# Half a head's scores inside the next half's query projection, and a new order of the routing's work on VectorE, in a product-key expert layer

## The chip, the cores and the metric

One Trainium2 chip, one core. The metric is the device time of one execution in microseconds (us). The kernel before takes 1438.37 us (median of three runs, 1434.36 to 1438.52).

## What is computed

One block for 512 tokens of width 1024, in float32: `h = x + W_out [gated MLP group ; chunked attention group](RMSNorm(x))`, then `out = h + PEER(RMSNorm(h))`. PEER is a layer of 16384 experts, of which each token uses 8 x 16. The routing is what the change touches:

```python
q = (xb @ w_query).reshape(PEER_TOKEN_BLOCK, PEER_HEADS, 2, PEER_HALF)
sc = jnp.einsum('thpd,hpkd->thpk', q, sub_keys).astype(jnp.float32)
s_top, i_top = lax.top_k(sc, PEER_TOPK)
cand = s_top[:, :, 0, :, None] + s_top[:, :, 1, None, :]
cand_idx = i_top[:, :, 0, :, None] * PEER_NKEYS + i_top[:, :, 1, None, :]
...
best, pos = lax.top_k(cand, PEER_TOPK)
eidx = jnp.take_along_axis(cand_idx, pos, axis=-1)
g = jax.nn.softmax(best, axis=-1)
...
return jnp.einsum('thk,thkd->td', (g * h.astype(jnp.float32)).astype(xb.dtype), vv)
```

There are 8 heads; a head has two halves, each with 128 sub-keys of length 128. For each token and half the 16 best sub-keys are taken, the 50 pairs that can be among the best 16 sums are formed, and the best 16 of these give the experts' numbers and the gates.

## The kernel before

**The whole.** Three of the four tiles of 128 tokens (384 tokens) go densely through all experts: TensorE multiplies every expert row, and a gating stage between the two products writes each token's gates at its experts. One tile, and 64 tokens of the last dense tile in the first product, fetch their experts' rows by indirect DMA instead. A float32 product is three products of split parts ("high" and "low"): `mm3`. Each weight block arrives as `raw` (512 KB, queue SP), ScalarE writes its high part `hi` (L151), and GpSimd or VectorE the low part `lo` (L152). There are 3 raw, 5 hi and 5 lo buffers, handed on in order, so a load and its splits can be at most a few blocks ahead of TensorE.

**Stages.** In the profile the routing runs from about 224 to 442 us, the gating stage to about 606, and the last stage, with the second expert product, to the end.

**The routing, loop over h = 0 to 8 (L863 and after).** `candidates(h)` (L803) projects the head's two halves, 24 products of 512 columns each (tile `pa` from `xbh`, `xbl`), and copies each half to SBUF on ScalarE (`qt`, L820). Then come the first of the head's fill tiles and the scores of both halves, 8 products of 128 columns on TensorE (L828), which ScalarE copies to `scr` (L831). A fill tile is 24 products of 320 columns for the first expert product (`pu`, `first_products`, L716 for its activation `act`, L713); the table FILL says how many a head gets, and they give TensorE something to do beside the choice. VectorE takes the top 16 of each half (`top16`, L729 to L733: three tiles of tokens, five instructions each).

One loop turn later follows head h - 1: `pairs` (L744) copies the first half's values and positions and adds the pairs (`cand`, L764); for all heads but the last two of these turns, ScalarE does the copies (L750, L756, L757). `choose` (L769) spreads the candidates' numbers into `tree` (L771, on ScalarE; on VectorE for the last two heads), takes the top 16 of the candidates, makes six bit masks of the positions (L778, one instruction for each bit) and picks with `COPY_PREDICATED` by each bit (L788), down to `eidx` (L790).

**Row products.** From h = 2 on, the chosen indices of head h - 2 go to GpSimd (`eui`, L665, L666), which issues indirect DMAs of expert rows, six at a time into six buffers `rowe` (L650). In the next turn VectorE multiplies each with the token row `xbu` (L659, 128 x 1024, with the sum to `du`). A buffer is free for the next gather when its product is done.

**The end of the routing.** Turn h = 8 has no projection but a "bridge" of 8 fill tiles. Then one further tile is multiplied and the digits of the chosen numbers, `ii` (L843 to L850, from the last `eidx`), are transposed on TensorE (L918), with which the gating stage begins: VectorE makes one-hots (`hb`, `lb` L929, `am` L948), GpSimd their products (`bm`, L940).

**What sets the order.** Outside of the gating stage a scheduler places the instructions of each engine in its queue, by the order in which the code names them and by their dependences; `issue_after` and `queued_behind` hold instructions behind a given one. The queues run in order: an instruction that waits holds up all behind it on its engine.

Of the kernel before, what the change touches and what calls it, by code (L numbers as in the profile page):

```python
# [8 lines left out]
F32 = mybir.dt.float32  # L9
# [10 lines left out]
P = 128  # L20
# [48 lines left out]
LAST = 2  # L69
HELD = 2  # L70
SOME = 15
FILL = (2, 2, 2, 2, 3, 3, 3, 3)
DELAY = 6
SLACK = 4
IDLE = (8, 5)
# [17 lines left out]
def hybrid_block(tc, x, ln1, w_in, gng, wsT, bsb, qkg, bias, w_out, ln2, wq, skT, uT, ud, vd, out):  # L93
    nc = tc.nc
    ctx = ExitStack()
    with ctx:
# [13 lines left out]
        def big(tag, dt, bufs):  # L110
# [2 lines left out]
        ident = const.tile([P, P], F32, name="ident")  # L113
        make_identity(nc, ident)
        iota_k = const.tile([P, P], F32, name="iota_k")
        nc.gpsimd.iota(iota_k, pattern=[[1, P]], base=0, channel_multiplier=0,
                       allow_small_or_imprecise_dtypes=True)

# [608 lines left out]
        def top16(val, pos, src, scratch):  # L727

            nc.vector.max(val[:, 0:8], src)  # L729
            nc.vector.max_index(pos[:, 0:8], val[:, 0:8], src)  # L730
            nc.vector.match_replace(scratch, val[:, 0:8], src, LOW)
            nc.vector.max(val[:, 8:16], scratch)
            nc.vector.max_index(pos[:, 8:16], val[:, 8:16], scratch)  # L733

        def keys(pool, n):

# [2 lines left out]

        def best_keys(pool, top, pos, u, p2, src):  # L740
            rep = pool.tile([P, NK], F32, name="rep", tag="rep", bufs=2)
            top16(top[:, 0, u, p2, :], pos[:, u, p2, :], src, rep)

        def pairs(pool, top, pos, n, ps=None, own=False):  # L744

# [23 lines left out]
        def choose(pool, cand, n, best, to, mask, tree, spread=nc.gpsimd.tensor_copy):  # L769
# [4 lines left out]
                rep = pool.tile([P, NCAND], F32, name="rep2", tag="rep2", bufs=2)  # L774
                top16(best[:, t, :], bpos[:, t, :], cand[:, 0, t, :], rep)

            for i in range(6):
                nc.vector.tensor_scalar(mask[:, i * n * TOPK:(i + 1) * n * TOPK], bpos.rearrange("p t k -> p (t k)"),  # L778
                                        1 << i, None, op0=ALU.bitwise_and)
# [10 lines left out]
            nc.vector.tensor_copy(to, tree[:, :, :, 0])  # L790

        def softmax(pool, best, n):
# [7 lines left out]
            nc.vector.reciprocal(zs, zs)  # L800
            nc.vector.tensor_tensor(best, ex, zs[:, :, None].to_broadcast(full), op=ALU.mult)

        def candidates(h):  # L803

            if h:
                w = chunk_of(wq, h, eng=nc.gpsimd)
            else:
                with queued_behind(behind_norm):
                    w = chunk_of(wq, h)
            skt = rq.tile([P, 2, NK], F32, name="skt", tag="skt", bufs=2)  # L810
            nc.sync.dma_start(skt, skT[:, 2 * h:2 * h + 2, :])
            top, pos = keys(rq, ND)
            qts = []
            for p2 in range(2):
                ps = pa()
                for k in range(KT):
                    mm3(ps, w(k, slice(p2 * P, (p2 + 1) * P)), (xbh[:, k, :], xbl[:, k, :]),
                        k == 0, k == KT - 1)
                qt = rq.tile([P, S], F32, name="qt", tag="qt", bufs=2)
                nc.scalar.copy(qt, ps)  # L820
                qts.append(qt)
            fill = first_products(sum(FILL[:h]) + BC, FILL[h], nc.gpsimd, True)
            next(fill, None)
            s0 = rq.tile([P, 2, NK], F32, name="s0", tag="s0", bufs=2)
            for p2 in range(2):
                sp = pa()
                for t in range(TT):
                    nc.tensor.matmul(sp[:, t * P:(t + 1) * P], qts[p2][:, t * P:(t + 1) * P],  # L828
                                     skt[:, p2, :], start=True, stop=True)
                sc = rq.tile([P, ND, NK], F32, name="scr", tag="scr", bufs=2)  # L830
                nc.scalar.copy(sc, sp.rearrange("p (t n) -> p t n", n=NK)[:, GT:, :])  # L831
                nc.scalar.copy(s0[:, p2, :], sp[:, 0:NK])
                for t in range(ND):
                    best_keys(rq, top, pos, t, p2, sc[:, t, :])
            nc.scalar.dma_start(s0d[h], s0.rearrange("p a n -> p (a n)"))
            for _ in fill:
                pass
            return top, pos


        def indices_of(t):
# [12 lines left out]
        for j in range(BC):  # L854
# [6 lines left out]
        cands = []  # L861
        for h in range(NH + 1):
            dots_early(0)  # L863
            if h < NH:
                cands.append(candidates(h))
            else:
# [7 lines left out]
            if h > 0:  # L874
# [350 lines left out]
```

## Time and profile before

| | before |
|---|---|
| median of three runs | 1438.37 us |
| the profiled execution | 1439.93 us |
| its span, first to last instruction | 1438.1 us |
| its mean granted TensorE clock | 0.990 |
| TensorE matmul busy | 1395.6 us (97%) |
| VectorE busy | 1160.8 us (81%) |
| GpSimd busy | 703.3 us (49%) |
| ScalarE busy | 612.3 us (43%) |

A span is the time from the first to the last instruction of the profiled execution, whose own time is a little longer. In the views that follow, PE is TensorE's matmuls, DVE VectorE, ACT ScalarE, POOL GpSimd, SP the queue of the weight loads. L828 is line 828 of the kernel. A row of the waits reads "engine, what, line <- what released it: us in total, times, longest". A row of a timeline reads "start us, duration us, engine, line, operation, out<-in, shape, count", and in brackets the idle time before it and what ended that. A row of stretches gives its length and each engine's busy time and count of instructions (PE, weight loads, DVE, ACT, POOL), then the granted clock (1.00 is full), the share of the DMA engines and GB/s. A row of groups gives count, busy us, mean ns of one, and the idle time before.

### The profile page before, as it was taken

Reading aid. Unit: us, or ns where it says so; the run is one execution under the profiler, and the core shown is the slowest. Engines: PE = TensorE matmul, PEld = TensorE weight load, DVE = VectorE, ACT = ScalarE, POOL = GpSimd, SP = SyncE. Lnnn points to the kernel's source line nnn. Section 1 sums busy time; section 2 is a strip of 40 time slices with the busy share of each in tenths; the row PEclk is TensorE's granted clock in tenths of the full one; section 3 lists DMA queues with packets and bytes.
Section 4 is the critical chain, followed back from the end, with each engine's and each line's share of the span. In section 5 each row is a group of like instructions: output and inputs, shape, how many; then the busy total and the mean of one; then the engine's idle time right before and its main releaser. Section 6 shows DMA issues by size and latency. Waiting matters only on the chain.

```text
span 1438.1 us, 21787 instructions
## 1 busy us (share of the span) xinstructions
PE 1395.6 (97%) x7838; PEld 1233.5 (86%) x7838; DVE 1160.8 (81%) x2558; ACT 612.3 (43%) x975; POOL 703.3 (49%) x479
## 2 busy tenths in 40 slices
PE   9999999999988897899999999999999999999998
PEld 7887788998988887899898899898998998888887
DVE  5537753688999989689999999899879888688883
ACT  5447635443433444554434444343433333333331
POOL 0002104588778897514454556556545455254520
PEclk9999999999999999999999999999999999999999
DMA  4452226478667997879799999999989989789981
GB/s 164 129 191 74 89 103 206 137 263 280 230 212 233 300 326 231 272 264 351 285 354 360 335 351 367 346 399 363 388 328 360 358 328 366 260 328 352 350 325 62
DMA packets 164331, 396.25 MB, mean 276 GB/s; under 512 B 12880, under 2 KB 75232, under 8 KB 162176
## 3 DMA queue, kind: packets, MB, share of 16 engines
q1 hardware_dynamic: 64640, 194.14, 37.6%
q0 software_dynamic: 48176, 173.46, 32.9%
q10 hardware_dynamic: 51408, 27.27, 6.5%
q8 instruction: 61, 1.00, 0.3%
q14 instruction: 46, 0.38, 0.1%
HBM read 363.34 MB, written 31.46 MB: 275 GB/s over the span
## 4 chain that ended last, share of the span: by engine, by line
PE 74%; DVE 13%; DMA 6%; ACT 3%; POOL 2%; issue 2%; POOLq 0%; ACTq 0%; DVEq 0%; SPq 0%
PE pa L1145 21%; PE px L1145 11%; PE pu L189 9%; PE pu L190 9%; PE pu L191 9%; PE pa L189 4%; PE pa L190 3%; PE pa L191 3%; DMA gd<-gst 3%; DVE lo L152 2%; PE pa L956 2%; DVE row L1086 1%; DVE am L948 1%; DMA gc<-gd 1%; DVE acc L1097 1%
## 5 line engine op out<-in xcount | busy, mean ns | idle before, releaser
L151 ACT ACTIVATE hi<-raw 128x1024 fp32r<-128x1024 f32 x296 | 312.5, 1058 | 443.7 <-DMA raw<-in_vd 116.0
L152 DVE TENSOR_TENSOR lo<-raw,hi 128x1024 fp32r<-128x1024 f32 x243 | 302.7, 1247 | 79.8 <-ACT hi L151 79.2
L1084 POOL DMA_INDIRECT row<-in_ud,eint x128 | 199.5, 1559 | 172.7 <-DVE acc L1097 107.4
L1095 POOL DMA_INDIRECT row<-in_vd,eint x128 | 185.6, 1450 | 172.3 <-DVE row L1086 120.7
L189 PE MATMUL pu<-xch,hi 128*128 128x320 f32 x784 | 247.5, 316 | 1.2 <-ACT act L713 1.2
L190 PE MATMUL pu<-xcl,hi 128*128 128x320 f32 x784 | 242.5, 309 | 0.0
L191 PE MATMUL pu<-xch,lo 128*128 128x320 f32 x784 | 242.1, 309 | 0.0
L1145 PE MATMUL pa<-hi,wh 128*128 128x512 f32 x512 | 199.8, 390 | 0.0
L1145 PE MATMUL pa<-lo,wh 128*128 128x512 f32 x512 | 199.3, 389 | 0.0
L152 POOL TENSOR_TENSOR lo<-raw,hi 128x1024 fp32r<-128x1024 f32 x53 | 126.5, 2405 | 92.9 <-ACT hi L151 92.1
L1097 DVE SCALAR_TENSOR_TENSOR acc<-row,hw,acc 128x1024 f32<-128x1024 f32 x128 | 164.9, 1288 | 1.4 <-DMA row<-in_vd,eint 1.2
L1086 DVE SCALAR_TENSOR_TENSOR row<-row,xb 128x1024 f32<-128x1024 f32 x128 | 157.5, 1233 | 2.3 <-DMA row<-in_ud,eint 2.3
L1145 PE MATMUL pa<-hi,wl 128*128 128x512 f32 x512 | 158.2, 389 | 0.0
L189 PEld LDWEIGHTS pu<-xch,hi 128*128 128x128 f32 x784 | 148.3, 189 | 4.3 <-ACT act L713 2.9
L190 PEld LDWEIGHTS pu<-xcl,hi 128*128 128x128 f32 x784 | 148.3, 189 | 1.5
L191 PEld LDWEIGHTS pu<-xch,lo 128*128 128x128 f32 x784 | 148.1, 189 | 0.0
L956 PE MATMUL pa<-bm,am 128*128 128x128 f32 x768 | 99.0, 282 | 16.4 <-DVE am L948 8.7
L1145 PEld LDWEIGHTS pa<-hi,wl 128*128 128x128 f32 x512 | 96.1, 188 | 20.4
L1145 PEld LDWEIGHTS pa<-hi,wh 128*128 128x128 f32 x512 | 96.1, 188 | 20.3
L1145 PEld LDWEIGHTS pa<-lo,wh 128*128 128x128 f32 x512 | 96.1, 188 | 20.1
L956 PEld LDWEIGHTS pa<-bm,am 128*128 128x128 f32 x768 | 94.1, 197 | 20.6 <-issue 9.1
L1145 PE MATMUL px<-hi,wh 128*128 128x512 f32 x256 | 100.7, 393 | 4.2 <-ACT hi L151 4.2
(236 smaller groups left out, 2661.1 us busy)
## 6 DMA issues: line engine op xcount, KB each, us to landing
raw<-in_uT SPq DMA_DIRECT2D x128, 512.0 KB, 5.6
raw<-in_vd SPq DMA_DIRECT2D x128, 512.0 KB, 6.1
gd<-gst ACTq DMA_DIRECT2D x24, 1024.0 KB, 7.5
gc<-gd SPq DMA_DIRECT2D x15, 1280.0 KB, 8.5
raw<-in_w_in SPq DMA_DIRECT2D x19, 512.0 KB, 4.4
raw<-in_wq SPq DMA_DIRECT2D x16, 512.0 KB, 3.6
raw<-in_w_out SPq DMA_DIRECT2D x8, 512.0 KB, 3.6
gc<-gd SPq DMA_DIRECT2D x15, 256.0 KB, 10.3
```

Of the source, the lines that this page charges most:

```text
L151: nc.scalar.activation(hi, raw, AF.Copy)
L152: ins = eng.tensor_tensor(lo, raw, hi.bitcast(F32), op=ALU.subtract)
L189: nc.tensor.matmul(ps, lh[0], rh[0], start=first, stop=False)
L190: nc.tensor.matmul(ps, lh[0], rh[1], start=False, stop=False)
L191: nc.tensor.matmul(ps, lh[1], rh[0], start=False, stop=last)
L948: nc.vector.tensor_tensor(am, iota_k[:, None, :].to_broadcast(full), g[:, 0, c * TC:(c + 1) * TC, None].to_broadcast(full), op=ALU.is_equal)
L956: nc.tensor.matmul(ps[:, i * P:(i + 1) * P], am[:, 4 * q + i, :], bm[:, 4 * q + i, :], start=True, stop=True)
L1084: nc.gpsimd.indirect_dma_start(out=row, out_offset=None, in_=ud, in_offset=bass.IndirectOffsetOnAxis(ap=eint[:, j:j + 1], axis=0))
L1086: nc.vector.scalar_tensor_tensor(row, row, 1.0, xb0, op0=ALU.mult, op1=ALU.mult, accum_out=hw[:, j:j + 1])
L1095: nc.gpsimd.indirect_dma_start(out=row, out_offset=None, in_=vd, in_offset=bass.IndirectOffsetOnAxis(ap=eint[:, j:j + 1], axis=0))
L1097: nc.vector.scalar_tensor_tensor(acc0, row, hw[:, j:j + 1], acc0, op0=ALU.mult, op1=ALU.add)
L1145: nc.tensor.matmul(accs[t][half], (wh, wh, wl)[k][:, b, tok], w[b][k % 2][:, ds_], start=first and k == 0, stop=last and k == 2)
```

## The change

Five edits, all in the routing.

1. Projection and scores are cut apart. `projected_keys(h, p2)` is a half's projection, which pauses in its middle, after 12 of its 24 products; there `best_of` of the half before is called: its scores (4 products), the copies to `scr` and `s0`, and its top 16. Only head 7's second half has no projection behind it; its scores stand behind head 7's first fill tile. `scr` gets four buffers instead of two.
2. The fill tiles become 0, 1, 2, 3, 4, 4, 3, 3 instead of 2, 2, 2, 2, 3, 3, 3, 3; the sum, 20, stays.
3. The six masks become one `TENSOR_TENSOR` of 128 x 288, positions AND a constant tile `bits` (six columns, filled on GpSimd at the start of the kernel). This holds for the choice in the last stage too.
4. The copies in `pairs` go to VectorE for every head. The spread copy into `tree` stays on ScalarE for the early heads.
5. The row products (`dots_early`) are named after `candidates(h)` instead of before it, and held behind the last instruction of the latest top 16 (`found`).

```diff
-FILL = (2, 2, 2, 2, 3, 3, 3, 3)
+FILL = (0, 1, 2, 3, 4, 4, 3, 3)
...
-            for i in range(6):
-                nc.vector.tensor_scalar(mask[:, i * n * TOPK:(i + 1) * n * TOPK], bpos.rearrange("p t k -> p (t k)"),
-                                        1 << i, None, op0=ALU.bitwise_and)
             mask = mask.rearrange("p (l t k) -> p l t k", t=n, k=TOPK)
+            nc.vector.tensor_tensor(mask, bpos[:, None, :, :].to_broadcast([P, 6, n, TOPK]),
+                                    bits[:, :, None, None].to_broadcast([P, 6, n, TOPK]), op=ALU.bitwise_and)
...
+        def projected_keys(h, p2):
...
+            for k in range(KT):
+                if k == KT // 2:
+                    yield
+                mm3(ps, weights_q[h](k, slice(p2 * P, (p2 + 1) * P)), (xbh[:, k, :], xbl[:, k, :]),
+                    k == 0, k == KT - 1)
+            qts[h, p2] = rq.tile([P, S], F32, name="qt", tag="qt", bufs=2)
+            nc.scalar.copy(qts[h, p2], ps)
...
+        def best_of(h, p2):
...
+            for t in range(ND):
+                ins = best_keys(rq, top, pos, t, p2, sc[:, t, :])
+            found[:] = [getattr(ins, "ins", ins)]
...
         def candidates(h):
...
             for p2 in range(2):
...
+                for _ in projected_keys(h, p2):
+                    if p2:
+                        best_of(h, 0)
+                    elif h:
+                        best_of(h - 1, 1)
             fill = first_products(sum(FILL[:h]) + BC, FILL[h], nc.gpsimd, True)
-            next(fill, None)
...
+            if h == NH - 1:
+                next(fill, None)
+                best_of(h, 1)
             for _ in fill:
                 pass
...
         for h in range(NH + 1):
-            dots_early(0)
             if h < NH:
-                cands.append(candidates(h))
-            else:
+                candidates(h)
+            with queued_behind(found):
+                dots_early(0)
+            if h == NH:
...
-                    cand = pairs(rq, *cands.pop(0), ND, ps[:, 6 * ND * TOPK:8 * ND * TOPK], h >= NH - 1)
+                    cand = pairs(rq, *top_pos.pop(h - 1)[:2], ND, ps[:, 6 * ND * TOPK:8 * ND * TOPK], True)
```

**What moves on TensorE.** Head 7 in the kernel before: the end of its second half's projection, its first fill tile (24 rows, of which the end stands here), and the scores of both halves in one row.

```order
L190 MATMUL pa<-xbl,hi 128x512
L191 MATMUL pa<-xbh,lo 128x512
L189 MATMUL pu<-xbh,hi 128x320
...
L190 MATMUL pu<-xbl,hi 128x320
L191 MATMUL pu<-xbh,lo 128x320
L828 MATMUL pa<-skt,qt 128x128 x8
L189 MATMUL pu<-xbh,hi 128x320
```

The middle of head 7's second projection in the changed kernel (its lines are 3 further down for the products):

```order
L192 MATMUL pa<-xbh,hi 128x512
L193 MATMUL pa<-xbl,hi 128x512
L194 MATMUL pa<-xbh,lo 128x512
L835 MATMUL pa<-skt,qt 128x128 x4
L192 MATMUL pa<-xbh,hi 128x512
L193 MATMUL pa<-xbl,hi 128x512
L194 MATMUL pa<-xbh,lo 128x512
```

The four scores of head 7's first half stand between the products of its second half. The same holds for every half but the last.

**What moves on VectorE at the end of the routing.** Before: from the last `COPY_PREDICATED` of head 7's choice to the first one-hots. `zs` and `ex` are the softmax's, `rowe` a gathered row.

```order
L788 COPY_PREDICATED tree<-pa,tree 128x48
L659 SCALAR_TENSOR_TENSOR rowe,du<-rowe,px 128x1024
L790 COPY eidx<-tree 128x3x16
...
L846 CAST ii<-eidx 128x128
...
L659 SCALAR_TENSOR_TENSOR rowe,du<-rowe,px 128x1024
L849 TENSOR_SCALAR ii<-ii 128x128
L659 SCALAR_TENSOR_TENSOR rowe,du<-rowe,px 128x1024
L850 CAST ii<-ii 128x384
L659 SCALAR_TENSOR_TENSOR rowe,du<-rowe,px 128x1024 x3
L929 TENSOR_TENSOR hb<-iota_k,pa 128x128
```

The same place in the changed kernel:

```order
L662 SCALAR_TENSOR_TENSOR rowe,du<-rowe,px 128x1024
L790 COPY_PREDICATED tree<-pa,tree 128x48x2
L662 SCALAR_TENSOR_TENSOR rowe,du<-rowe,px 128x1024
L790 COPY_PREDICATED tree<-pa,tree 128x48
L662 SCALAR_TENSOR_TENSOR rowe,du<-rowe,px 128x1024
L792 COPY eidx<-tree 128x3x16
L867 CAST ii<-eidx 128x128
L868 TENSOR_SCALAR ii<-ii 128x128
L869 TENSOR_SCALAR ii<-ii 128x128
L870 TENSOR_SCALAR ii<-ii 128x128
L871 CAST ii<-ii 128x384
L950 TENSOR_TENSOR hb<-iota_k,pa 128x128
```

The last row products moved from between and behind the `ii` instructions to between those of head 7's choice. Counted back to head 7's first top 16, three groups of six row products stand ahead of `ii` now.

**What moves on GpSimd.** Turn h = 4 before: the casts of `xbh` and `xbl` (`xch`, `xcl`), eight gathers, and the low parts of the weights.

```order
L152 TENSOR_TENSOR lo<-raw,hi 128x1024
L887 COPY xch<-xbh 128x2560
L650 DMA rowe<-in_ud,eui 128x1024 x8
L888 COPY xcl<-xbl 128x2560
L152 TENSOR_TENSOR lo<-raw,hi 128x1024 x2
```

The same turn in the changed kernel, with the indices `eui` ahead:

```order
L155 TENSOR_TENSOR lo<-raw,hi 128x1024 x4
L668 DMA eui<-eidx 64x8
L669 CAST eui<-eidx 64x8
L908 COPY xch<-xbh 128x2560
L909 COPY xcl<-xbl 128x2560
L653 DMA rowe<-in_ud,eui 128x1024 x6
L155 TENSOR_TENSOR lo<-raw,hi 128x1024 x6
```

Between two low parts there now stand the indices, both casts and six gathers. Before, it was both casts and eight gathers, with the indices one low part earlier.

More of the change, by code (lines that the diff above doesn't have):

```diff
@@ L115, in hybrid_block @@
         iota_k = const.tile([P, P], F32, name="iota_k")
+        bits = const.tile([P, 6], U32, name="bits")
+        for i in range(6):
+            nc.gpsimd.memset(bits[:, i:i + 1], 1 << i)
         nc.gpsimd.iota(iota_k, pattern=[[1, P]], base=0, channel_multiplier=0,
@@ L732, in top16 @@
             nc.vector.max(val[:, 8:16], scratch)
-            nc.vector.max_index(pos[:, 8:16], val[:, 8:16], scratch)
+            return nc.vector.max_index(pos[:, 8:16], val[:, 8:16], scratch)
         def keys(pool, n):
@@ L741, in best_keys @@
             rep = pool.tile([P, NK], F32, name="rep", tag="rep", bufs=2)
-            top16(top[:, 0, u, p2, :], pos[:, u, p2, :], src, rep)
+            return top16(top[:, 0, u, p2, :], pos[:, u, p2, :], src, rep)
         def pairs(pool, top, pos, n, ps=None, own=False):
@@ L801, in softmax @@
             nc.vector.tensor_tensor(best, ex, zs[:, :, None].to_broadcast(full), op=ALU.mult)
-        def candidates(h):
-            if h:
-                w = chunk_of(wq, h, eng=nc.gpsimd)
-            else:
[L808 to L813, printed above, removed]
-            for p2 in range(2):
[L815 to L821, printed above, removed]
-            fill = first_products(sum(FILL[:h]) + BC, FILL[h], nc.gpsimd, True)
-            next(fill, None)
[L824 to L835, printed above, removed]
@@ new lines, in hybrid_block @@
+        weights_q, top_pos, qts, found = {}, {}, {}, []
+        def projected_keys(h, p2):
+            if p2 == 0:
+                if h:
+                    weights_q[h] = chunk_of(wq, h, eng=nc.gpsimd)
+                else:
+                    with queued_behind(behind_norm):
+                        weights_q[h] = chunk_of(wq, h)
+            ps = pa()
+            for k in range(KT):
[5 more added lines that the diff above has]
+            nc.scalar.copy(qts[h, p2], ps)
@@ new lines, in best_of @@
+        def best_of(h, p2):
+            if p2 == 0:
+                skt = rq.tile([P, 2, NK], F32, name="skt", tag="skt", bufs=2)
+                nc.sync.dma_start(skt, skT[:, 2 * h:2 * h + 2, :])
+                s0 = rq.tile([P, 2, NK], F32, name="s0", tag="s0", bufs=2)
+                top_pos[h] = (*keys(rq, ND), skt, s0)
+            top, pos, skt, s0 = top_pos[h]
+            qt = qts.pop((h, p2))
+            sp = pa()
+            for t in range(TT):
+                nc.tensor.matmul(sp[:, t * P:(t + 1) * P], qt[:, t * P:(t + 1) * P],
+                                 skt[:, p2, :], start=True, stop=True)
+            sc = rq.tile([P, ND, NK], F32, name="scr", tag="scr", bufs=4)
+            nc.scalar.copy(sc, sp.rearrange("p (t n) -> p t n", n=NK)[:, GT:, :])
+            nc.scalar.copy(s0[:, p2, :], sp[:, 0:NK])
+            for t in range(ND):
+                ins = best_keys(rq, top, pos, t, p2, sc[:, t, :])
+            found[:] = [getattr(ins, "ins", ins)]
+            if p2:
+                nc.scalar.dma_start(s0d[h], s0.rearrange("p a n -> p (a n)"))
@@ L836, in candidates @@
+        def candidates(h):
+            for p2 in range(2):
+                for _ in projected_keys(h, p2):
+                    if p2:
+                        best_of(h, 0)
+                    elif h:
+                        best_of(h - 1, 1)
+            fill = first_products(sum(FILL[:h]) + BC, FILL[h], nc.gpsimd, True)
+            if h == NH - 1:
+                next(fill, None)
+                best_of(h, 1)
             for _ in fill:
                 pass
-            return top, pos
@@ L860, in hybrid_block @@
                 activate_tile()
-        cands = []
         for h in range(NH + 1):
-            dots_early(0)
             if h < NH:
-                cands.append(candidates(h))
-            else:
+                candidates(h)
+            with queued_behind(found):
+                dots_early(0)
+            if h == NH:
                 for i, _ in enumerate(first_products(sum(FILL) + BC, BRIDGE, nc.gpsimd, True)):
```

## The prediction

> **What bounds the kernel now.** I read the page first, then what TensorE waits for: inside the routing, and from the gating stage's end on.
>
> ```profile
> PE 1395.6 (97%) x7838; PEld 1233.5 (86%) x7838; DVE 1160.8 (81%) x2558; ACT 612.3 (43%) x975; POOL 703.3 (49%) x479
> ...
> PE 74%; DVE 13%; DMA 6%; ACT 3%; POOL 2%; issue 2%; POOLq 0%; ACTq 0%; DVEq 0%; SPq 0%
> ```
> ```profile
> PE pu L189 <- ACT act L713: 5.6, 2, 3.4
> PE pa L828 <- ACT qt L820: 3.3, 1, 3.3
> ```
> ```profile
> PE pu L189 <- ACT act L713: 1.2, 2, 0.9
> ```
>
> TensorE is busy 97% of the span, and after 627 it waits 1.2 us in all (the last fence). So a microsecond that TensorE is ahead at the end of the routing is still ahead at the end of the program, and what the change can win there is what TensorE loses inside the routing (224 to 442, middle fence): 5.6 + 3.3 = 8.9 us of waits in three places. Each has ScalarE as the releaser; two are ScalarE standing in the split of a raw weight that has not landed.
>
> ```profile
> 343.45 1.06 ACT L151 ACTIVATE hi<-raw 128x1024 fp32r<-128x1024 f32 x1 [4.41 <-DMA raw<-in_wq]
> ```
> ```profile
> 403.10 1.06 ACT L151 ACTIVATE hi<-raw 128x1024 fp32r<-128x1024 f32 x1 [7.12 <-DMA raw<-in_uT]
> ```
>
> A wait is dearer than its length. These stretches begin right after the three waits (3.3, 2.2 and 3.4 us), and PEclk is the granted clock:
>
> ```profile
> 345.00:351.00 6.00, 5.97 (x25) 5.97 (x26) 2.75 (x7) 2.71 (x8) 5.37 (x5) 0.52 0.97 367
> 404.60:408.60 4.00, 4.00 (x18) 4.00 (x19) 4.00 (x28) 1.38 (x2) 2.80 (x3) 0.60 0.34 110
> 431.00:434.50 3.50, 3.50 (x24) 3.50 (x25) 3.36 (x9) 1.10 (x2) 3.13 (x3) 1.00 0.90 300
> ```
>
> The last runs at full clock: 24 products of 320 columns in 3.50 us, 0.146 us each, 3.5 us a tile. By that pitch the first stretch lost 6.0 - 25 x 0.146 = 2.3 us and the second 4.0 - 18 x 0.146 = 1.4 us. In all the routing gives away 8.9 + 3.7 = 12.6 us, 5.6 of them (3.3 + 2.3) before head 7. That is the most that the change can win here.
>
> **Part by part: TensorE.** No matmul is added. Half a head's scores move into the middle of the next half's projection, so the copy of the projected half (qt) has 2.7 us of matmuls over it, where the old place had one fill tile, 3.5 us, for both halves. The new fills (0,1,2,3,4,4,3,3) have the old sum. Two head starts without a fill between them give the pitch of the wide products:
>
> ```profile
> 238.67 1.78 PE pa L828 x16
> 258.40 1.78 PE pa L828 x16
> ```
>
> (19.73 - 1.78 - 48 x 0.146) / 48 = 0.228 us, so a head's projection is 48 x 0.228 = 10.9 us, and half a head's scores 0.9. I take the three old waits as gone: each half's copy now has those 2.7 us over it, ScalarE loses the pair copies, on whose inputs it stood, and the exp moves one fill later. That is -12.6, if nothing new waits.
>
> **A new wait on GpSimd.** Its order in head 4 is now: last fill's low part, indices, both casts of x, six gathers, and only then the low part of head 5's query weights.
>
> ```profile
> L152 POOL TENSOR_TENSOR lo<-raw,hi 128x1024 fp32r<-128x1024 f32 x45 | 107.5, 2408 | 59.8 <-ACT hi L151 59.1
> L650 POOL DMA_INDIRECT rowe<-in_ud,eui x43 | 41.2, 958 | 12.3 <-issue 9.5 <-POOL eui L666 0.8 <-PE pu L191 0.6
> L665 POOL DMA_DIRECT2D eui<-eidx x8 | 4.5, 562 | 18.8 <-DVE top L729 13.4 <-DVE gate L729 3.5 <-DVE eidx L790 1.8
> L888 POOL CAST xcl<-xbl 128x2560 fp32r<-128x2560 f32 x1 | 2.3, 2327 | 0.0
> ...
> L666 POOL CAST eui<-eidx 64x8 int32<-64x8 f32 x8 | 1.5, 188 | 1.8 <-issue 1.5
> ```
>
> Each gather is 0.96 and 0.3 of issue. 2.4 + 0.8 (indices) + 2 x 2.3 + 6 x 1.26 + 2.4 = 17.8 us, behind a high part of 1.06 on ScalarE: 18.9. That can start when head 4's projection has used its first query weight for the last time, at three quarters or so (9.1 of 10.9 us), and TensorE reaches head 5 after the rest, 1.8, and scores and four fills, 1.8 + 14.0: 17.6 later. So TensorE waits 1.3 there; raw loads may add (the split of 343.45 waited 4.4), and I take 1.8, between 1.3 and, if the clock drops after it as after the 2.2 us wait (1.4 to 2.3 more), 4.
>
> By the Trainium skill (TensorE: Matmul & The Clock Gate, "What's actually happening") the clock halves only after an idle window of about 3.4 us; by that rule this wait costs no clock and the sum stands as below; by the row it could be 1.4 to 2.3 worse. The trace does not agree with the rule: 2.2 us were followed by a clock of 0.60, 3.4 us by 1.00.
>
> **VectorE: the term that decides.** Early in the routing it waits for scores and rows, so what is added there is free:
>
> ```profile
> DVE top L729 <- ACT scr L831: 31.0, 3, 16.5
> DVE rowe L659 <- DMA rowe<-in_ud,eui: 9.9, 7, 3.8
> ```
>
> Not at the end. TensorE's last routing step, the transposes of the index digits (L918), needs ii, which needs the last head's choice, and the new order on VectorE puts everything else ahead of it: all 18 row products that are left when head 7's first scores come (before, three of the last six stood behind ii). I add it up from these marks:
>
> ```profile
> 405.30 0.47 DVE L729 MAX8 top<-scr 128x8 f32<-128x128 f32 x2
> ...
> 412.18 0.24 DVE L764 TENSOR_TENSOR cand<-top,pa 128x96 f32<-128x96 f32 x1
> ...
> 414.86 0.31 DVE L729 MAX8 gate<-cand 128x8 f32<-128x50 f32 x2
> ...
> 423.65 1.75 DVE L771 COPY tree<-cand 128x1536 f32<-128x1536 f32 x1
> ...
> 425.32 0.08 DVE L730 MATCH_VALUE_LOAD bpos<-gate,cand 128x8 f32 x1
> ...
> 427.49 1.43 DVE L778 TENSOR_SCALAR pa<-bpos 128x48 uint32<-128x48 uint32 x6
> ...
> 434.06 0.25 DVE L790 COPY eidx<-tree 128x48 f32<-128x48 f32 x1
> ...
> 440.20 0.35 DVE L850 CAST ii<-ii 128x384 f32<-128x384 int32 x1
> ```
> ```profile
> L778 DVE TENSOR_SCALAR pa<-bpos 128x48 uint32<-128x48 uint32 x48 | 10.0, 209 | 0.9
> ```
> ```profile
> 441.61 1.21 DVE L659 SCALAR_TENSOR_TENSOR rowe<-rowe,px 128x1024 f32<-128x1024 f32 x1
> ...
> 442.75 1.21 DVE L659 SCALAR_TENSOR_TENSOR rowe<-rowe,px 128x1024 f32<-128x1024 f32 x1
> ```
> ```profile
> L929 DVE TENSOR_TENSOR lb<-iota_k,pa 128x256 f32<-128x256 f32 x5 | 2.1, 414 | 0.0
> ```
>
> One row product takes 1.15 us of VectorE, from the two starts in the third fence.
>
> - both halves of head 7's top-16: 405.3 to 412.2, 6.9 us
> - pairs and spread copy of head 6: to 414.9, 2.7
> - choice of head 6 mixed with head 7's pairs: to 423.65, 8.8; its six masks (209 ns each, of which I count 0.13 as own time in this mix: 0.8) become one of 288 columns, which I price as the compare of 256 columns, 0.45: 8.4
> - spread copy of head 7: to 425.3, 1.7
> - choice of head 7, with the softmax's first step: to 434.06, 8.7, less a row product in it, and 0.45 in place of the masks' 1.43: 6.6
> - the softmax's rest and ii: to 440.55, 6.5, less two row products: 4.2
> - 18 row products: 20.7
>
> Sum 51.2. To this 1 us for rows or the exp that come late (0 to 4: a wait for rows was up to 3.8).
>
> When does it start? Head 7's projection starts here, and the transposes stood here:
>
> ```profile
> 378.93 0.39 PE L189 MATMUL pa<-xbh,hi 128*128 128x512 f32 x1
> ```
> ```profile
> 441.56 0.49 PE L918 MATMUL pa<-ident,ii 128*128 128x128 f32 x3
> ```
>
> 378.9 - 5.6 (losses gone) + 1.8 (new wait) - 0.9 (head 6's second scores come later) = 374.2; 0.9 + 36 x 0.228 later, at 383.3, come head 7's first scores; 1.8 for them and their copy: 385.1. With 51.2 + 1.0, ii is there at 437.3, the transposes at 437.5. TensorE, without waiting, would be there at 441.6 - 12.6 + 1.8 = 430.8. So it waits **6.7 us at L918 for ii**, and after so long a wait the first fill goes at half clock: 2.0 more (between the 2.3 and 1.4 above).
>
> Sum: -12.6 + 1.8 + 6.7 + 2.0 = **-2.1**. Behind it the gating stage follows TensorE's second fill, through ScalarE:
>
> ```profile
> 445.72 0.44 ACT L713 ACTIVATE act<-pu 128x320 f32<-128x320 f32 x1 [3.52 <-PE pu L191]
> 446.05 2.00 ACT L151 ACTIVATE hi<-raw 128x1024 fp32r<-128x1024 f32 x2
> ```
>
> so its own long wait shifts with the rest. In the last stage the choice of the gathered tile gets the merged mask too, eight times; TensorE waits 1.2 us there in all, so that cover makes it nothing (bounds -1 to +2, VectorE having no share in those 1.2). The gating stage's wait also bears on the merged mask:
>
> ```profile
> 448.03 2.38 POOL L152 TENSOR_TENSOR lo<-raw,hi 128x1024 fp32r<-128x1024 f32 x1
> 450.37 1.92 POOL L940 TENSOR_TENSOR bm<-hb,lb 128x1024 f32<-128x1024 f32 x1
> ```
> ```profile
> 448.08 5.30 DVE L152 TENSOR_TENSOR lo<-raw,hi 128x1024 fp32r<-128x1024 f32 x1 [1.27 <-ACT hi L151]
> ```
> ```profile
> L152 DVE TENSOR_TENSOR lo<-raw,hi 128x1024 fp32r<-128x1024 f32 x1 | 1.2, 1219 | 0.0
> ```
>
> VectorE's low part, two operands from SBUF, takes 1.22 alone (last fence) and took 5.30 while GpSimd ran two such instructions. The old mask read SBUF once; the new one reads bpos and bits there. GpSimd has eight low parts of 2.4 us in the tail's 51, so a mask meets one with 0.38 and then waits 1.2 in the mean, up to 2.4; of the two masks on the tail that is 0.9 (0 to 4.8). The sum is **-1.2**.
>
> The Trainium skill (SBUF — State Buffer, "Who interferes with whom") speaks against this edit: such a VectorE instruction and a GpSimd one that reads SBUF lock each other out for the whole instruction. If both masks meet a low part's full length, the sum is -2.1 + 4.8 = +2.7 by it; the 5.30 agrees with the rule, and only how often they meet is open.
>
> The profiled execution took 1439.93 (span 1438.1); by the sum the changed one takes 1438.7. The median, 1438.37, is 1.6 below that execution, so the median should be **1437.2**.
>
> **The rivals.**
>
> *The tail does not bind* (0.33). If VectorE's tail is shorter than 51.2 (row products in stretches where it waits anyway, or head 4's rows done earlier), each microsecond off it is one off the end, down to 430.8 at the transposes: -12.6 + 1.8 = -10.8, 1427.6; with half of the wait gone and no slow clock -12.6 + 1.8 + 3.4 = -7.4, 1431. Also here: since hb now stands right behind ii, GpSimd's low part could be over before VectorE's begins, and part of the 5.30 goes, some 1 to 4 us. For it: VectorE has 41 us of waits early in the routing. Against: in the mark rows, from 405 on, it has none.
>
> *GpSimd holds up the weights* (0.15): gathers now wait for row slots, which wait for row products, which wait for a half's top-16, and the low parts queue behind them. It decides once a head waits over 6 us in sum before head 7's first scores, where each microsecond delays the tail too. Two more heads with the wait of 1.8 and a slow clock of 2.0 each: 2 x 3.8 = 7.6, so -1.2 + 7.6 = +6.4, 1445. For it: GpSimd is near full in heads 4 to 6. Against: five split buffers of lead.
>
> *The masks wait* (0.07): both of the tail meet a low part and the instruction behind it, 5.30 - 1.22 twice: -2.1 + 8.2 = +6.1, 1444.5.
>
> *The change doesn't do what it says*: the order shows it does; only the waits for raw weights may stay, since the ScalarE copies still stand behind those splits. Then part of the 12.6 stays, and the tail's wait at L918 shrinks by as much: no change in the sum. This lies in my forecast (0.45).
>
> **How the numbers follow.** About 0.3%, 4.3 us, is what a measurement of this kernel can tell from no change. The forecast with its bounds (stall 1.3 to 4, late rows 0 to 4) spans -3 to +4, "same". Of the first rival's 0.33 nearly all lies beyond 4.3 below: faster 0.32. Of the two rivals that cost time 0.2: slower. Same 0.48. The range takes the first rival to its full gain, and the other two nearly to their ends: 1427 to 1445.
>
> **What would show it.** Right: a new row of waits "L918's line on ii" of 4 to 10 us, gone rows for qt and act, a slow clock after 438, and TensorE at the gating products about where it was (450). Wrong: no wait there and transposes before 433; or new waits for GpSimd's low parts in heads 3 to 7; or a mask row with a mean of over 1 us.

## The result and the profile after

The changed kernel takes 1462.25 us (median of four runs, 1458.80 to 1463.67) against 1437.92 for the kernel before (median of four): 24 us slower by these medians. The ratio on record is 1.0144, with a 95% interval of 1.0116 to 1.0172, a little less than the 1.017 of the two medians; against 1440.95, the median of all 29 runs of the kernel before in this case, the loss is 21 us. The forecast was 1437.2, no change, with a range of 1427 to 1445.

The profiled execution took 1458.8, its span is 1456.7. First the page's busy times and its chain, as for the kernel before:

```profile
PE 1405.4 (96%) x7838; PEld 1240.0 (85%) x7838; DVE 1188.8 (82%) x2496; ACT 612.1 (42%) x957; POOL 702.3 (48%) x485
...
PE 63%; DVE 21%; DMA 8%; issue 3%; ACT 2%; POOL 2%; another core or an unknown queue 0%; ACTq 0%; POOLq 0%; DVEq 0%; SPq 0%
```

VectorE has 62 instructions fewer and is busy 28 us longer (1160.8 before), and its share of the chain went from 13% to 21%. What TensorE waits for in the routing:

```profile
PE pa L835 <- issue: 11.3, 4, 4.5
PE pu L192 <- ACT act L716: 3.6, 1, 3.6
PE pa L939 <- DVE ii L871: 2.5, 1, 2.5
PE pa L194 <- POOL lo L155: 2.1, 1, 2.1
PE pu L194 <- POOL lo L155: 0.5, 1, 0.5
```

The first row is new and is the largest: the scores (L835), four times, up to 4.5 us, "issue" meaning that the view names no releaser. The wait for ii that the prediction put at 6.7 us is 2.5, because TensorE itself is late. The transposes (L939) stand 16.4 us later than before (441.56):

```profile
458.00 0.56 PE L939 MATMUL pa<-ident,ii 128*128 128x128 f32 x2 [2.54 <-DVE ii L871]
```

So 16.4 of the 18.6 us between the two profiled spans are lost inside the routing. The gating stage takes as long as before (168.6 against 168.5, from the transposes to the last stage's first product); the last stage takes 830.1 against 828.0, which was not traced.

Most of VectorE's 28 us are in one line. The merged masks, those of the routing first, then those of the last stage (minimum, median and maximum in ns):

```profile
L781 DVE TENSOR_TENSOR pa<-bpos,bits x8: 463/5242/6125, 252.7 to 445.8; 128x288 uint32<-128x288 uint32 x8
L781 DVE TENSOR_TENSOR mask<-bpos,bits x8: 240/255/264, 639.0 to 900.6; 128x96 uint32<-128x96 uint32 x8
```

In the routing an undisturbed one takes 463 ns, the 0.45 that was priced; the median is 5.24 us. The eight take 32.2 us in sum, 28.5 more than eight times 0.463; the 48 small masks of before took 10.0. In the last stage GpSimd has no low parts, and no mask is long. One of the long masks on VectorE, then GpSimd around it (the first of six gathers, and the low parts behind them), then TensorE's scores:

```profile
297.44 6.11 DVE L781 TENSOR_TENSOR pa<-bpos,bits 128x288 uint32<-128x288 uint32 x1 [0.87 <-DVE bpos L736]
303.65 1.23 DVE L790 COPY_PREDICATED tree<-pa,cand 128x864 f32<-128x864 uint32 x1
304.92 2.83 DVE L790 COPY_PREDICATED tree<-pa,tree 128x768 f32<-128x768 uint32 x5
```
```profile
288.82 1.02 POOL L653 DMA_INDIRECT rowe<-in_ud,eui  x1 [0.54 <-DVE rowe L662]
...
296.13 7.09 POOL L155 TENSOR_TENSOR lo<-raw,hi 128x1024 fp32r<-128x1024 f32 x3
```
```profile
307.85 0.62 PE L835 MATMUL pa<-skt,qt 128*128 128x128 f32 x2 [3.59 <-issue]
```

The mask began 1.3 us into a run of three low parts on GpSimd (296.13 to 303.22) and ended 0.33 us behind the last of them. It was held to the end of the run, not to that of the one low part that it met. Then the five last `COPY_PREDICATED` of that head end at 307.75, and 0.1 us later TensorE's scores begin. They wait for a PSUM tile: `pa` is a ring of four, a head takes five (two projections, two scores, one for the masks), and the mask's tile comes free with the choice's last instruction. The same 0.1 us lies between the two at 339.37, 369.12 and 398.75. The waits over 2.5 us are followed by a low clock (third number from the right), 0.57 and 0.50 of full speed:

```profile
307.90:311.90 4.00, 4.00 (x15) 3.52 (x16) 3.90 (x26) 0.65 (x2) 3.48 (x4) 0.57 0.43 133
398.80:402.80 4.00, 4.00 (x14) 3.52 (x15) 3.90 (x26) 0.65 (x2) 3.14 (x3) 0.50 0.04 5
```

### The profile page after: what moved, and what is told of

It is laid out like the page before. It is cut to its first block, busy times and chain, and to the rows that moved or that the text cites. A ratio compares the mean times of both kernels' runs of the same rounds, so it can differ in the third digit from the quotient of the medians.

```text
span 1456.7 us, 21703 instructions
## 1 busy us (share of the span) xinstructions
PE 1405.4 (96%) x7838; PEld 1240.0 (85%) x7838; DVE 1188.8 (82%) x2496; ACT 612.1 (42%) x957; POOL 702.3 (48%) x485
## 4 chain that ended last, share of the span: by engine, by line
PE 63%; DVE 21%; DMA 8%; issue 3%; ACT 2%; POOL 2%; another core or an unknown queue 0%; ACTq 0%; POOLq 0%; DVEq 0%; SPq 0%
PE pa L1166 19%; PE px L1166 10%; PE pu L194 7%; PE pu L192 7%; PE pu L193 7%; DVE rowe L662 3%; DMA gd<-gst 3%; PE pa L192 3%; PE pa L977 2%; PE pa L193 2%; PE pa L194 2%; DVE lo L155 2%; DVE tree L790 2%; DVE pa L781 2%; DVE acc L1118 1%
## 5 line engine op out<-in xcount | busy, mean ns | idle before, releaser
L155 DVE TENSOR_TENSOR lo<-raw,hi 128x1024 fp32r<-128x1024 f32 x243 | 299.2, 1233 | 80.0 <-ACT hi L154 77.5
L1105 POOL DMA_INDIRECT row<-in_ud,eint x128 | 202.8, 1585 | 190.7 <-DVE acc L1118 129.2
L1116 POOL DMA_INDIRECT row<-in_vd,eint x128 | 180.3, 1408 | 158.1 <-DVE row L1107 105.3
L1166 PE MATMUL pa<-lo,wh 128*128 128x512 f32 x512 | 199.9, 390 | 0.0
L1166 PE MATMUL pa<-hi,wh 128*128 128x512 f32 x512 | 199.6, 390 | 0.0
L1166 PE MATMUL pa<-hi,wl 128*128 128x512 f32 x512 | 158.4, 389 | 0.0
L1166 PEld LDWEIGHTS pa<-hi,wh 128*128 128x128 f32 x512 | 96.4, 188 | 20.8
L1166 PEld LDWEIGHTS pa<-lo,wh 128*128 128x128 f32 x512 | 96.2, 188 | 20.4
L1166 PEld LDWEIGHTS pa<-hi,wl 128*128 128x128 f32 x512 | 96.1, 188 | 20.2
L1166 PE MATMUL px<-hi,wh 128*128 128x512 f32 x256 | 100.6, 393 | 3.2 <-DMA raw<-in_vd 3.2
```

The lines of the kernel that those rows point to most:

```text
L155: ins = eng.tensor_tensor(lo, raw, hi.bitcast(F32), op=ALU.subtract)
L1105: nc.gpsimd.indirect_dma_start(out=row, out_offset=None, in_=ud, in_offset=bass.IndirectOffsetOnAxis(ap=eint[:, j:j + 1], axis=0))
L1116: nc.gpsimd.indirect_dma_start(out=row, out_offset=None, in_=vd, in_offset=bass.IndirectOffsetOnAxis(ap=eint[:, j:j + 1], axis=0))
L1166: nc.tensor.matmul(accs[t][half], (wh, wh, wl)[k][:, b, tok], w[b][k % 2][:, ds_], start=first and k == 0, stop=last and k == 2)
```

## The experiments

Theory M: the merged mask loses the time, because its two operands in SBUF let GpSimd's low parts block it. Rival G: the new order (scores inside the projections, row products, gathers ahead of low parts) loses it. All ratios are to the kernel before, with 95% intervals.

**E1. The merged mask alone, in the kernel before.**

```diff
 (before.py)
...
-                nc.vector.tensor_scalar(mask[:, i * n * TOPK:(i + 1) * n * TOPK], ...)
...
+            nc.vector.tensor_tensor(mask, bpos[:, None, :, :].to_broadcast([P, 6, n, TOPK]),
+                                    bits[:, :, None, None].to_broadcast([P, 6, n, TOPK]), op=ALU.bitwise_and)
```

> The kernel before with the merged mask alone. Theory M (the merged mask reads two operands from SBUF and stands still while GpSimd runs low parts; 4.0 us each in the changed kernel where an undisturbed one took 0.46): the masks of this kernel too take 2 to 6 us each where a low part runs, some 3 of them lie on VectorE's last 45 us, and the time rises by 5 to 15 us. Theory G (GpSimd's new order and the new place of the scores make the loss, the mask is a by-product): the mask rows stay near 0.5 us here, or cost nothing, and the time stays within 4 us of before.

Measured: 1449.82, 1.0085 (1.0059 to 1.0110). The size is as theory M has it, the masks aren't:

```profile
L781 DVE TENSOR_TENSOR pa<-bpos,bits x8: 461/468/6194, 270.3 to 435.9; 128x288 uint32<-128x288 uint32 x8
```

Only two of eight were blocked (6.19 and 2.50 us); together they took 7.8 us more than two undisturbed ones. So this run left open whether the blocking makes the loss of this edit in the old order; E8, E11 and E12 bear on it.

**E2. The changed kernel with the six masks of before.** E1's diff backwards, in the changed kernel.

> The changed kernel with the six masks of before, the other four edits kept. Theory M: the waits of the scores (11.3 us) go, and the time falls from 1462 to what the prediction had without the mask, 1434 to 1441. Theory G: the waits of the scores stay, and the time stays above 1452.

Measured: 1445.97, 1.0038 (1.0019 to 1.0057), 16 us less than the changed kernel, 5 more than theory M's upper bound. GpSimd's and ScalarE's instructions of the routing stand in the changed kernel's order. The waits of the scores are gone; what is left is, among others, the wait for ii that was forecast, and one for a low part:

```profile
PE pa L940 <- DVE ii L872: 4.6, 1, 4.6
PE pu L194 <- POOL lo L155: 4.4, 1, 4.4
```

**E3. The merged mask with one operand in PSUM.** Nothing else is changed; the six columns are copied once a head into the free part of the mask's own PSUM tile.

```diff
 (after.py)
+                bits_ps = ps[:, 8 * ND * TOPK:8 * ND * TOPK + 6].bitcast(U32)
+                nc.vector.tensor_copy(bits_ps, bits)
...
-                                    bits[:, :, None, None].to_broadcast([P, 6, n, TOPK]), op=ALU.bitwise_and)
+                                    bits_of[:, :, None, None].to_broadcast([P, 6, n, TOPK]), op=ALU.bitwise_and)
```

> The changed kernel with the merged mask kept, but its second operand in PSUM: six columns of the same PSUM tile, copied there once a head, so that the mask reads SBUF only once. Theory M: every mask takes about 0.5 us, and the time is that of the six masks or up to 4 us less, 1430 to 1441. If the length of the mask came from its shape or operation and not from the second SBUF operand, it stays at 4 us and the time above 1452.

Measured: 1438.20, 0.9996 (0.9976 to 1.0016). The whole loss of 24 us is gone, with the mask still one instruction of the same shape. Its times, and TensorE's waits in the routing and at the start of the gating stage:

```profile
L781 DVE TENSOR_TENSOR pa<-bpos,pa x8: 455/461/464, 254.0 to 426.8; 128x288 uint32<-128x288 uint32 x8
```
```profile
PE pu L194 <- POOL lo L155: 4.4, 1, 4.4
PE pa L979 <- POOL bm L963: 2.4, 1, 2.4
PE pu L192 <- ACT act L716: 1.7, 2, 1.3
PE pa L194 <- POOL lo L155: 1.5, 1, 1.5
PE pa L941 <- DVE ii L871: 1.3, 1, 1.3
```

No mask is over 0.464 us, though six of the eight begin inside a run of low parts here too. GpSimd's and ScalarE's instructions of the routing stand in the same order as in the changed kernel, so it is not a new order that brought the time back. It was the second SBUF operand. This is the rule that the prediction drew from the Trainium skill (SBUF — State Buffer, "Who interferes with whom"): a VectorE instruction with two SBUF inputs and a GpSimd one that reads SBUF lock each other out. The trace agrees, 0.46 against up to 6.1 us; that a mask waits for more than the one instruction it met goes beyond the rule (last section). Rival G, the new order by itself, is out for the 24 us.

**E4. Six masks, and the row products named ahead of the projection, as before.**

```diff
 (E2's kernel)
+            dots_early(0)
             if h < NH:
                 candidates(h)
-            with queued_behind(found):
-                dots_early(0)
```

> The changed kernel with the six masks, and with the row products named ahead of the head's projection again, as before. By the prediction's tail (18 row products ahead of the last index digits) the products behind the top 16 cost about 6 us at the end, so this kernel should be 2 to 6 us faster than the one with six masks alone. If the tail does not bind, the two are within 2 us, or this one is slower since VectorE waits for rows ahead of the top 16 again.

Measured: 1447.56, 1.0064 (1.0041 to 1.0087): not faster than E2, rather slower, with intervals that overlap. The old place brings back what it had cost: VectorE waits for rows (first row), and TensorE behind ScalarE (second). By the expectation this is the case in which the tail does not bind. But TensorE loses those 13.2 us ahead of the tail here and never waits for ii, so the run doesn't test the tail; E7 and E9 do.

```profile
DVE rowe L662 <- DMA rowe<-in_ud,eui: 13.3, 7, 4.1
```
```profile
PE pu L192 <- ACT act L716: 13.2, 5, 8.0
```

**E5. The scores' PSUM tile from the other pool**, the mask left in SBUF as changed.

```diff
 (after.py)
-            sp = pa()
+            sp = pu()
```

> The changed kernel, merged mask in SBUF and all, with one edit: the scores' PSUM tile comes from the two-buffer pool of the fill tiles (pu) instead of the four-buffer ring pa, in which one tile holds the mask until the choice's last COPY_PREDICATED. Theory R (the long mask reaches TensorE through that ring, 13.4 us of waits at the scores): those waits go, and some 5 to 15 of the 24 us with them. Theory D (VectorE's added 28 us reach the end through ii in any case): the waits of the scores go, but TensorE then waits as much longer at the transposes for ii, and the time falls by less than 4 us.

Measured: 1444.66, 1.0024 (0.9995 to 1.0053), 18 us less than the changed kernel, more than the 5 to 15 of theory R and far from theory D's. Of the waits at the scores (11.3 us by the view above, not the expectation's 13.4) 2.8 are left, behind ScalarE and not behind the ring, and ii is waited for 3.8. But the masks are shorter too (second fence):

```profile
PE pa L939 <- DVE ii L871: 3.8, 1, 3.8
...
PE pu L835 <- ACT qt L822: 1.6, 1, 1.6
PE pu L835 <- ACT act L716: 1.2, 1, 1.2
```
```profile
L781 DVE TENSOR_TENSOR pa<-bpos,bits x8: 460/2224/2419, 248.0 to 428.1; 128x288 uint32<-128x288 uint32 x8
```

12.8 us in sum instead of 32.2: five of them now wait for the end of one low part, and none is passed by at a boundary. The edit also changed the order of gathers and low parts on GpSimd. So the 18 us belong to the ring and to the way masks and low parts met, together; how much of them is the ring alone, this run cannot say.

**E6. The kernel before with E3's mask.**

```diff
 (E1's kernel)
+                bits_ps = ps[:, 8 * ND * TOPK:8 * ND * TOPK + 6].bitcast(U32)
+                nc.vector.tensor_copy(bits_ps, bits)
```

> The kernel before with the merged mask alone, its second operand in PSUM. If the loss of the same edit with both operands in SBUF (1449.8 against 1439.9) is the blocking by GpSimd's low parts, this kernel is at 1434 to 1441, with every mask near 0.46 us. If merging the masks itself costs (one late instruction in place of six that are mixed with others), it stays near 1446 to 1450.

Measured: 1450.47, 1.0073 (1.0046 to 1.0100). All masks take 0.46, and still it is slow, but the run does not answer the question. The copy of the six columns stands in VectorE's queue, and ScalarE, which copies the pairs into the same tile, waited for it:

```profile
ACT pa L753 <- DVE pa L881: 19.1, 4, 7.0
```

**E7. E3 with the low parts of the last two tiles ahead of the last gathers.**

```diff
 (E3's kernel)
                     behind.append(done[0])
+                for _ in range(HELD):
+                    split_next()
             if h > 1:
```

> The kernel with the mask's second operand in PSUM, and the low parts of the last two tiles of the routing named ahead of the last indices and gathers on GpSimd. There TensorE waited 4.4 us for a low part that stood behind an index copy which waits for six gathered rows. If that wait was a loss of its own, the time falls by 3 to 6 us, to about 1433 to 1436, below the kernel before. If VectorE's tail binds as the prediction has it, TensorE only comes to the transposes sooner and waits there for ii instead (1.3 us now, 5 then): no change within 2 us; and the last six rows come later, which may cost 1 to 3.

Measured: 1441.39, 1.0010 (0.9993 to 1.0026): 3 us more than E3 and no change against the kernel before, as the prediction's tail has it. The wait for the low part is gone, and TensorE stands at the transposes for ii instead, from 430.74 to 440.73:

```profile
PE pa L941 <- DVE ii L871: 10.0, 1, 10.0
```
```profile
441.00:444.50 3.50, 3.50 (x18) 3.50 (x18) 2.49 (x7) 0.00 (x0) 1.39 (x1) 0.64 0.49 150
```

**E8. E6 with the columns copied on ScalarE** for the heads whose pair copies are there.

```diff
 (E6's kernel)
-                nc.vector.tensor_copy(bits_ps, bits)
+                (nc.vector.tensor_copy if h >= NH - 1 else nc.scalar.copy)(bits_ps, bits)
```

> As the kernel before with the merged mask's second operand in PSUM, but the six columns are copied there on ScalarE for the heads whose pair copies are on ScalarE. On VectorE that copy stood ahead of ScalarE's copies into the same tile, which waited 19 us for it in sum, so that run did not test the mask. If the loss of the merged mask alone (1449.8) is blocking by GpSimd, this kernel is at 1434 to 1442. If it is still at 1446 or more, merging the six masks costs by the order that follows from it, in the kernel before, and blocking is not needed for that loss.

Measured: 1449.05, 1.0066 (1.0044 to 1.0088), with every mask at 0.46. On GpSimd the routing's instructions stand in E1's order, one by one. So in the old kernel the merging costs 9 us without any blocking. GpSimd shows how, then ScalarE and TensorE's wait:

```profile
393.00 0.94 POOL L653 DMA_INDIRECT rowe<-in_ud,eui  x1 [0.30 <-issue]
393.94 0.60 POOL L668 DMA_DIRECT2D eui<-eidx  x1
399.09 0.19 POOL L669 CAST eui<-eidx 64x8 int32<-64x8 f32 x1 [4.55 <-DMA rowe<-in_ud,eui]
...
403.32 2.34 POOL L155 TENSOR_TENSOR lo<-raw,hi 128x1024 fp32r<-128x1024 f32 x1
```
```profile
410.07 1.06 ACT L154 ACTIVATE hi<-raw 128x1024 fp32r<-128x1024 f32 x1 [13.53 <-DMA raw<-in_uT]
```
```profile
PE pu L192 <- ACT act L716: 12.2, 1, 12.2
```

With one instruction in place of six the scheduler orders GpSimd's queue otherwise in several places; in this one it puts an index copy in the middle of six gathers instead of ahead of them. The copy writes `eui`, which the three gathers in flight still read, and it waits for their landing (4.55 us); three low parts stand behind it, three raw buffers stay taken, the high part of the same weight begins 7 us later than before (410.07 against 403.10), and TensorE waits. The profiled execution is the fastest of the six, 1441.13, so the 9 us are the median's and not this profile's. E1's profile, of an execution of 1448.70, has the same stall in ScalarE and TensorE:

```profile
414.37 1.06 ACT L154 ACTIVATE hi<-raw 128x1024 fp32r<-128x1024 f32 x1 [13.14 <-DMA raw<-in_uT]
```
```profile
PE pu L192 <- ACT act L716: 13.3, 3, 9.8
```

**E9. E7 with the last six row products behind ii**, spread over the first steps of the gating stage.

```diff
 (E7's kernel)
         ready_early(NH - 1)
-        dots_early(0)
...
-            gather_early(1, gat, ROWA)
             multiply_tile()
...
+                    dots_early(ROWA - 1)
                     gather_early(1, gat, ROWA)
-                dots_early(LAGE)
+                dots_early(max(LAGE, ROWA - 1 - n))
```

> The kernel with the mask's second operand in PSUM and the held tiles' low parts first, in which TensorE came to the transposes at 430.7 and waited 10.0 us there for ii; here the last six row products (6.9 us of VectorE) stand behind ii, spread over the first four steps of the gating stage. If VectorE's tail of row products is what holds ii, ii comes 6 to 7 us sooner, TensorE waits 3 to 4 us, and the time falls by 3 to 7 us, to 1433 to 1438. If the gating stage has no room on VectorE (it is busy 28 of its first 38 us, 39 of the next 40), the products only move the loss: waits for one-hots grow by as much, no change within 2 us.

Measured: 1435.53, 0.9967 (0.9952 to 0.9983), 6 us under E7. The transposes come 7.4 us sooner than in E7, with a wait of 0.3:

```profile
433.37 0.55 PE L940 MATMUL pa<-ident,ii 128*128 128x128 f32 x3 [0.27 <-DVE ii L871]
```

In the profiled execution the gating stage takes most of that back (the last stage's first product, L1166 of the changed kernel, is at 603.73 against 605.40 in E7), so the profile shows 2 us of the gain, the medians 6. It also shows a stall that the forward moves brought into the last stage: TensorE waits for a low part on VectorE, which stands in a top 16 whose scores have not landed.

```profile
762.62 0.64 PE L194 MATMUL pu<-xch,lo 128*128 128x320 f32 x1 [3.35 <-DVE lo L155]
```
```profile
DVE top L732 <- DMA sc<-s0d: 6.0, 2, 3.6
```

**E10. E9 with two buffers for those scores.**

```diff
 (E9's kernel)
-            sc = ep.tile([P, n, 2, NK], F32, name="sc0", tag="sc0", bufs=1)
+            sc = ep.tile([P, n, 2, NK], F32, name="sc0", tag="sc0", bufs=2)
```

> The fastest kernel so far (mask operand in PSUM, held low parts first, last six row products in the gating stage), with two buffers instead of one for the scores of the gathered tile in the last stage (sc0). There it lost 3.35 us at 759, where VectorE stood in a top 16 whose scores had not landed (3.6 us) with a low part behind it that TensorE waits for, and 1 to 2 us of clock after that. If that is the loss, the time falls by 3 to 6 us, to 1430 to 1433 beside a before of 1440. If VectorE only waits for something else there, it stays at 1435 to 1437.

Measured: 1430.03, 0.9937 (0.9916 to 0.9959): faster than both kernels, 32 us below the changed one. The stall at 759 and the row of waits for these scores are gone; from the last stage's start to the end it takes 829.0 us against 833.2 in E9. So this edit accounts for some 4 us. In these two profiles the transposes, which lie ahead of it, also stand 3.7 us apart (the row below against 433.37), though VectorE, ScalarE and GpSimd have the routing's instructions in the same order: E9's profiled execution waited 3.0 us for a low part in front of head 5, and this one 0.5.

```profile
429.72 0.55 PE L940 MATMUL pa<-ident,ii 128*128 128x128 f32 x3 [0.33 <-DVE ii L871]
```

**E11 and E12. The kernel before, merged mask, and a turn's gathers held behind its index copy**; E11 with the operand in PSUM (E8's kernel), E12 with it in SBUF (E1's kernel).

```diff
+            copied[:] = [getattr(ins, "ins", ins)]
...
+                    with queued_behind(copied):
+                        gather_early(EARLY, gat, ROWA)
-                    gather_early(EARLY, gat, ROWA)
```

> The kernel before with the merged mask, its second operand in PSUM (1449), and with a turn's gathers held behind that turn's index copy on GpSimd. With the merged mask the scheduler had put three of six gathers ahead of the copy, which then waited 4.6 us for their landing with three low parts behind it; ScalarE then waited 13.5 us for a raw weight, TensorE 12.2. If that order is what the merging costs in the kernel before, this kernel is at 1437 to 1442, equal to before. If not, it stays at 1446 or more.

> The same, with the mask's second operand in SBUF as in the change. The difference to the kernel with the operand in PSUM is what GpSimd's blocking alone costs in the old order: 2 to 8 us (two of eight masks were blocked there, by 7.8 us in sum) if those masks are again blocked and near VectorE's critical stretch; nothing if they fall where VectorE waits anyway.

Measured: E11 1437.76, 0.9990 (0.9964 to 1.0016); E12 1436.23, 0.9978 (0.9957 to 1.0000). Both losses of the merging in the old kernel, E1's and E8's, are gone with GpSimd's order. The edit moves the gathers of every turn, and it was not run in the kernel before without the merging, so a gain of its own, which would hide part of the loss, is not excluded. In E12 five of the eight masks are blocked again, mildly:

```profile
L782 DVE TENSOR_TENSOR pa<-bpos,bits x8: 458/1162/2122, 270.9 to 424.9; 128x288 uint32<-128x288 uint32 x8
```

Masks blocked for up to 2.1 us cost nothing there. As far as these runs tell, what made E1 slow was the order on GpSimd (E8 has it, without a blocked mask, and is as slow), and not the mechanism that makes the changed kernel slow, although the same edit brings both.

## Why the prediction was wrong

**The step that failed** is the price of the merged mask: "a mask meets one with 0.38 and then waits 1.2 in the mean, up to 2.4; of the two masks on the tail that is 0.9 (0 to 4.8)". Three things in it were off.

- How often: six of eight masks met a low part. They do not meet by chance: a row product frees a row buffer, GpSimd's gather waits for that, and the low parts wait behind six gathers and then run back to back, while VectorE comes to the mask 3.2 to 3.5 us behind its last product (heads 2 to 5). That the new place of the products sets this step is argued from the order, not tried; in the old place two of eight were blocked in E1 and five in E12, of these seven only one (6.19) for longer than 2.50 us.
- How long: up to 6.1 us, since a waiting mask can stay blocked through several low parts. The row that the prediction had, 5.30 us beside two GpSimd instructions, said so; the bound of 2.4 treated it as one.
- Which masks count: the prediction took the six early ones as free, because VectorE waits early in the routing. But the mask's PSUM tile is in the ring from which the scores take theirs, so a late choice stops TensorE, at the first scores of heads 4 to 7. That ring is not in the prediction at all. E3 (24 us back with the operand alone) shows the mask as the cause, E5 (18 us back with the scores' pool) that the loss passes through the ring and the runs of low parts, in shares that it leaves open.

The rival "the masks wait" had the right row and the right sign, with 0.07 for it, and was priced at 8.2 us for two masks instead of 28.5 on VectorE for eight.

**What held.** Without the blocking (E3, E7) the rest of the sum can be read step by step. The old waits go: in E7 TensorE comes to the transposes at 430.7, where the prediction had 430.8. (Of the two slow stretches in that sum the first lost nearer 2.7 us than 2.3: eight of its 25 products are scores of 128 columns, which take 0.10 us each at full clock and not 0.146.) The new wait in front of head 5 was put at 1.8 and is 1.5 in E3, with a clock of 1.00 after it; in E9's profile it is 3.0, with 0.56 after it, so the upper bound of 4 had its use. The wait for ii was put at 6.7 and is 10.0 in E7, because ii comes at 440.7 and not 437.3. Its start was right: head 7's first scores stand at 383.25, forecast 383.3. The tail itself, 52.2 with its late rows, took 55.6 from the forecast's 385.1, of them 2.7 in a wait for a row. A slow clock follows it, 0.64 over 3.5 us, a loss of 0.9 against 2.0. So -12.6 + 1.5 + 10.0 + 0.9 is about 0, and E3 and E7 measured 0.9996 and 1.0010. The gain of the four other edits is spent in the wait for ii, as forecast; that VectorE's row products hold ii is shown by E9, where moving six of the 18 brought ii 7 us sooner.

**What was not in it.** Merging six small instructions changes GpSimd's order in the kernel before and costs 9 us there without blocking (E8); another order gives them back (E11). The prediction priced the edit as VectorE time.

**What stays open.** E2 is 8 us slower than E3 by the medians, while six masks take 5 us more of VectorE than one and its copy; the rest was not traced. The last stage is 2 us longer in the changed kernel's profile, where the prediction had nothing (-1 to +2). The gating stage, from the transposes to the last stage's first product, lasts 160 (E2) to 170 us (E9) in these profiles; it takes back most of E9's start, and its own limit was not looked for.

## What to carry to other kernels

Before merging small VectorE instructions into one with two SBUF operands, look at what GpSimd runs at that time: if its instructions stand back to back, the merged one can wait for the whole run, and moving one operand to PSUM removed that here for a copy of 0.18 us. Price a longer instruction by what its buffer holds up, not only by its engine's idle time: a PSUM ring ties an engine that has time to one that has none. And when an instruction count changes under a scheduler, compare the order on the other engines too, since a copy that lands between transfers that read its target waits for all of them.

## What the runs showed of the hardware

- A VectorE instruction blocked by GpSimd can be passed by at the boundary between two GpSimd instructions: in the run of three (296.13 to 303.22) it began in the first and ended behind the third. The mask of 271.10, which began in the second of three, was let in behind it and took 2.49 us, and three of E5's masks behind the first of two or three; what decides it is open. The low parts themselves kept their 2.4 us. A gather does not block: the mask of 445.80 began while GpSimd issued one (445.00 to 445.94) and took 0.46.
- The same mask with one operand in PSUM took 455 to 464 ns in all eight places, beside the same low parts. In the seven kernels that have it so (E3, E6 to E11) none of 56 masks took longer than 464 ns.
- Waits of TensorE of 1.5 (E3) and 2.1 us (the changed kernel) left the clock at 1.00, those of 2.5 to 4.5 us in the changed kernel were followed by 0.50 to 0.57 over 3.5 to 4 us; in the kernel before 2.2 us was followed by 0.60 and 3.4 us by 1.00. The length of a wait alone does not tell it.
